# Rows of tokens fetched from DRAM by lists instead of products with one-hot matrices, in the expert loop of a decoder step

## The chip, the cores and the metric

One core of a Trainium2 chip runs the whole kernel. The metric is the device time of one execution in microseconds (us). A core's engines named below are PE (TensorE, the matrix engine), DVE (VectorE), ACT (ScalarE), POOL (GpSimd) and SP (SyncE, which here issues the weights' DMA transfers).

## What is computed

One layer of a hybrid decoder over 288 tokens (256 of a prompt, 32 of samples) of 1024 numbers: a mixer (a convolution and a state-space branch), a layer norm, a mixture of experts and a last layer norm. The change lies in the mixture of experts:

```python
def moe(h, w_r, b_r, w1, b1, w2, b2):
    t = h.reshape(-1, D_MODEL)
    logits = (t @ w_r + b_r).astype(jnp.float32)
    top_val, top_idx = lax.top_k(logits, TOP_K)
    gates = jax.nn.softmax(top_val, axis=-1)
    comb = jnp.einsum('tk,tke->te', gates,
                      jax.nn.one_hot(top_idx, N_EXPERTS, dtype=jnp.float32)).astype(h.dtype)
    out = jnp.zeros_like(t)
    for e in range(N_EXPERTS):
        gu = t @ w1[e] + b1[e]
        g = jnp.minimum(gu[:, :D_FF], SWIGLU_LIMIT)
        up = jnp.clip(gu[:, D_FF:], -SWIGLU_LIMIT, SWIGLU_LIMIT)
        act = g * jax.nn.sigmoid(SWIGLU_ALPHA * g) * (up + 1.0)
        out = out + comb[:, e:e + 1] * (act @ w2[e] + b2[e])
    return out.reshape(shp)
```

All data are float32. An expert's weights are 12 MiB, all experts' 384 MiB. The kernel computes an expert only for the tokens that chose it; 288 tokens with 4 experts each make 1152 pairs of token and expert.

## The kernel before

The first 330 us or so compute the mixer, the norm, `h2` (the tokens' rows after the second modulation, 288 rows of 1024 numbers, in three tiles of 128 partitions) and the router. For each expert the router leaves `posm` (a token's place in the expert's list, or a number that no place has), `comb` (its gate) and `cnt` (how many tokens the expert has).

Then comes the loop over 32 experts `e`, in `moe`. PE, DVE, ACT and POOL run the order in which the code is written. A group `b` is 32 tokens of an expert. The count is loaded into a register of each engine, and nested branches (`rest`) run as many groups as the expert has.

- **Gather** (`onehot`, `gather_mm`, `gather_tr`). DVE compares places with `iota` and makes a one-hot matrix `S` (128 x 3 x 64). PE multiplies `S` by `h2`: six float32 products of 512 columns into PSUM tile `ga`, which the trace shows as 12 records on line L1146. ACT copies `ga` to `gs`, PE transposes it with four products (`gt`, L1157), and ACT copies to `ht0`. This is 64 tokens, so two groups. Groups 2 and 3, and 4 and 5, each have a further gather (`S_1`, `S_2`, into `ht1`) inside the branch.
- **ff1** (`ph1`, L1174 and L1180): groups 1 and up first, inside the branches, then group 0. Tiles `w_0` to `w_7` are the first matrix.
- **Scatter** of the pair of experts before (`sc`, `ss`, L1245 and L1254), only at even `e`.
- **ff2** of groups 1 and up inside the second set of branches (`ph2`, L1209, tiles `w_8` to `w_11`).
- At the expert's end, in this order on PE: gather products of expert `e + 1`, at even `e` the transposes of the gates (`gp`, L1235), transposes `at` of the activations of group 0, transposes `gt` of the gathered rows, ff2 of group 0.
- **Gates** (`gates_a`, `gates_b`): DVE makes a one-hot matrix for a pair of experts in two operations (L1227, L1228), PE transposes it (`gp`) and ACT copies it to `gst`, the left side of the scatter. An expert with three groups or more has such a matrix for its further tokens too (`gp_x`, `gst_x`).

SP issues the weights in the order of use, 1 MiB a transfer, into a ring of 18 buffers (19 later): each transfer waits until PE has done with the tile that lay there (`done`, L1124 for `w_0` to `w_7`, L1126 for the others).

## Time and profile before

| what | before |
|---|---|
| median of 3 runs | 1525.32 us (1520.22 to 1526.88) |
| the profiled execution | 1517.3 us |
| its span, first to last instruction | 1515.2 us |
| PE busy in the span | 1225.3 us (81%) |
| DVE, ACT, POOL busy | 507.8, 336.1, 225.5 us |
| mean granted clock of PE | 0.938 of full speed |
| DMA, mean over the span | 308 GB/s |

The span leaves out what lies before the first and after the last instruction, 2.1 us in the profiled execution. The median of the runs is 8.0 us above the profiled execution. In the trace the expert loop begins at about 326 us with the first gather, its first ff1 product is at 337 us, and its last product is near 1497 us; the rest is the last norm. A row of a timeline gives start, duration, engine, line, operation, output and inputs, sizes, the number of records in it, and in brackets how long the engine sat idle before it and what released it. PEq, DVEq and ACTq are the engines' sequencers: the engine waited at a branch.

### The profile page before, as it was taken

Reading aid. Unit: us, or ns where it says so; the run is one execution under the profiler, and the core shown is the slowest. Engines: PE = TensorE matmul, PEld = TensorE weight load, DVE = VectorE, ACT = ScalarE, POOL = GpSimd, SP = SyncE. Lnnn points to the kernel's source line nnn. Section 1 sums busy time; section 2 is a strip of 40 time slices with the busy share of each in tenths; the row PEclk is TensorE's granted clock in tenths of the full one; section 3 lists DMA queues with packets and bytes.
Section 4 is the critical chain, followed back from the end, with each engine's and each line's share of the span. In section 5 each row is a group of like instructions: output and inputs, shape, how many; then the busy total and the mean of one; then the engine's idle time right before and its main releaser. Section 6 shows DMA issues by size and latency. Waiting matters only on the chain. (4 is left out here: it accounts for less than half of the span.)

```text
span 1515.2 us, 25944 instructions
## 1 busy us (share of the span) xinstructions
PE 1225.3 (81%) x10487; PEld 577.8 (38%) x10487; DVE 507.8 (34%) x910; ACT 336.1 (22%) x703; POOL 225.5 (15%) x181
## 2 busy tenths in 40 slices
PE   4888779967877888879889887788777998788885
PEld 1777668932222233323232332223222242323332
DVE  6799897742202212213122221022211131212233
ACT  3634655421111111111110110111111121111112
POOL 4676955411000000000000000000000000000022
PEclk9999898997999899999999998999989999999998
DMA  9456557468999998886982589998999549985582
GB/s 393 152 223 162 198 181 271 172 229 352 401 412 414 415 415 327 330 337 255 415 335 105 231 341 413 413 416 360 416 412 414 236 186 416 389 358 235 210 321 79
DMA packets 84660, 467.36 MB, mean 308 GB/s; under 512 B 8728, under 2 KB 10096, under 8 KB 45456
## 3 DMA queue, kind: packets, MB, share of 16 engines
q1 hardware_dynamic: 81264, 459.68, 76.4%
q8 instruction: 172, 2.82, 0.7%
q10 hardware_dynamic: 2912, 3.46, 0.7%
q0 software_dynamic: 224, 0.68, 0.3%
q14 instruction: 88, 0.72, 0.1%
HBM read 460.69 MB, written 3.10 MB: 306 GB/s over the span
## 5 line engine op out<-in xcount | busy, mean ns | idle before, releaser
L1382 POOL TENSOR_TENSOR acc.344_2930<-acc.344_2930,w_1.1848_32253 128x1024 f32<-128x1024 f32 x2 | 5.0, 2521 | 1097.1 <-DVEq L1299 1097.1
L1215 ACT COPY ysp.360_2947<-y 32x256 f32<-32x256 f32 x152 | 55.1, 362 | 125.6 <-PE y L1209 112.7
L1174 PE MATMUL gu<-b1h.19_79,sel.17_76 96*32 96x512 bf16 x220 | 22.6, 399 | 70.2 <-PEq L1299 45.2
L1198 ACT COPY at1.355_2942<-at 128x256 f32<-128x256 f32 x32 | 11.9, 372 | 217.4 <-PE at L1196 217.4
L565 DVE SCALAR_TENSOR_TENSOR v.103_626<-cb.73_323,pk.20_88,v.103_626 128x256 f32<-128x256 f32 x60 | 54.6, 911 | 1.5
L1174 PEld LDWEIGHTS <-sel.17_76 96*32 96x32 bf16 x220 | 7.0, 93 | 97.2 <-issue 96.1
L1251 DVE TENSOR_TENSOR acc.344_2930<-acc.344_2930,sc 128x512 f32<-128x512 f32 x60 | 39.8, 684 | 11.9 <-PE sc L1245 11.9
L1251 DVE TENSOR_TENSOR acc.344_2930<-acc.344_2930,sc_x 128x512 f32<-128x512 f32 x28 | 19.3, 688 | 28.1 <-PE sc_x L1245 28.1
L1215 DVE COPY ysp.360_2947<-y 32x256 f32<-32x256 f32 x24 | 10.2, 423 | 40.2 <-ACT ysp.360_2947 L1215 40.2
L1215 DVE COPY ysx.361_2948<-y 32x256 f32<-32x256 f32 x22 | 9.3, 421 | 38.6 <-ACT ysx.361_2948 L1215 38.6
L1158 ACT COPY ht0.358_2945<-gt 128x512 f32<-128x512 f32 x32 | 18.7, 585 | 10.0 <-PE gt L1157 9.9
L1198 ACT COPY at2.356_2943<-at 128x256 f32<-128x256 f32 x14 | 5.2, 372 | 61.9 <-PE at L1196 53.1
L1196 PEld LDWEIGHTS at<-consts.1_57,acts1.349_2936 128*128 128x128 f32 x64 | 6.4, 140 | 27.1 <-issue 27.1
L1196 PE MATMUL at<-consts.1_57,acts0.348_2935 128*128 128x128 f32 x64 | 13.4, 292 | 2.0 <-DVEq L1299 2.0
L1196 PEld LDWEIGHTS at<-consts.1_57,acts0.348_2935 128*128 128x128 f32 x64 | 7.5, 146 | 19.3 <-issue 16.4
L1196 PE MATMUL at<-consts.1_57,acts1.349_2936 128*128 128x128 f32 x64 | 14.0, 301 | 0.0
L1167 DVE TENSOR_SCALAR acts0.348_2935<-gu 128x256 f32<-128x256 f32 x32 | 13.2, 414 | 0.0
L1215 ACT COPY ysx.361_2948<-y 32x256 f32<-32x256 f32 x22 | 8.0, 362 | 22.4 <-PE y L1209 16.9
L1198 ACT COPY at0.354_2941<-at 128x256 f32<-128x256 f32 x32 | 12.3, 383 | 1.5 <-PE at L1196 1.5
L148 ACT COPY yx.131_1005<-y 32x288 f32<-32x288 f32 x10 | 6.9, 688 | 15.7 <-DVE yx.131_1005 L148 10.7
L1245 PE MATMUL sc_x<-ysx.361_2948,gst_x.1801_31355 128*128 128x512 f32 x8 | 6.5, 983 | 4.4 <-PEq L1299 4.4
L1245 PE MATMUL sc_x<-ysx.361_2948,gst_x.1851_32347 128*128 128x512 f32 x8 | 6.7, 1013 | 3.4 <-PEq L1299 3.4
(3185 smaller groups left out, 3004.6 us busy)
## 6 DMA issues: line engine op xcount, KB each, us to landing
wada_0.21_90<-in_w_ada_dram SPq DMA_DIRECT2D x1, 1024.0 KB
wada_1.22_92<-in_w_ada_dram SPq DMA_DIRECT2D x1, 1024.0 KB
wada_2.24_96<-in_w_ada_dram SPq DMA_DIRECT2D x1, 1024.0 KB
wada_3.25_98<-in_w_ada_dram SPq DMA_DIRECT2D x1, 1024.0 KB, 12.7
wada_4.26_100<-in_w_ada_dram SPq DMA_DIRECT2D x1, 1024.0 KB
wada_5.27_102<-in_w_ada_dram SPq DMA_DIRECT2D x1, 1024.0 KB
wada_6.28_104<-in_w_ada_dram SPq DMA_DIRECT2D x1, 1024.0 KB, 19.1
wada_7.29_106<-in_w_ada_dram SPq DMA_DIRECT2D x1, 1024.0 KB
```

What stands on the lines that cost most here:

```text
L148: (e.copy if e is nc.scalar else e.tensor_copy)(out, in_)
L565: V.scalar_tensor_tensor(vt_(j), cb[:, j, k:k + 256], wd[:, k, j:j + 1], vt_(j), op0=ALU.mult, op1=ALU.add)
L1158: nc.scalar.copy(ht, tp)
L1167: nc.vector.tensor_scalar(a, g[:, 256:512], -7.0, 7.0, op0=ALU.max, op1=ALU.min)
L1174: nc.tensor.matmul(o, sel[0:96, e:e + 1].to_broadcast([96, w]), b1v[0:96, :, c, :], start=True, stop=False, tile_position=tp)
L1196: nc.tensor.transpose(tp[:, o:o + P], a[:, h * P:h * P + P], ident)
L1198: nc.scalar.copy(t, tp[:, 256 * m:256 * m + 256])
L1215: (nc.vector.tensor_copy if q % 2 and b else nc.scalar.copy)(ys[r:r + 32, s], y[i, 0:256])
L1245: nc.tensor.matmul(sc, gst[0:W, t * P:t * P + P], ys[0:W, n * 512:n * 512 + 512], start=True, stop=True)
L1251: nc.vector.tensor_tensor(a, a, sc, op=ALU.add)
L1382: nc.gpsimd.tensor_tensor(acc[:, t], acc[:, t], g[:, 0], op=ALU.mult)
```

## The change

The tokens' rows are no longer gathered by products with one-hot matrices. At the end of the mixer `h2` is written to DRAM (`h2d`, three transfers issued by POOL). `lists` makes, with three products of 4 or 2 moving columns and three to five small DVE operations, a table `tab`: for each place its token's number (512, which is out of bounds, where the place is empty) and its gate. `fetch` is one indirect transfer of POOL that reads the rows of `h2d` named by the table, 128 places of 4 KB each; places out of bounds are to be skipped.

A fetch into `gs` serves the first 64 tokens of two experts, an even one and the odd one after it: it is issued at the end of the even expert before, and its rows are transposed (`columns`, 8 products, two copies) at the end of the odd expert before. A fetch into `gsx` serves tokens 64 to 191 of one expert: it is issued for every expert, between `ph1` and `ph2` of the expert before, and `columns_x` transposes 64 of its rows where the further gathers stood. The first pair of experts has no such fetch: it is still gathered by products, now six of 512 columns with a one-hot matrix of 128 places.

The gates' matrix is one DVE compare of `iota` with the table's token numbers, multiplied by the table's gate (`gates`); its transposes and copy are gone. POOL now loads the count and runs all branches too. `gs`, `gsx` and `htx` lie where `h2` lay. The function `more`, for over 192 tokens, is changed as well; no expert has that many here.

```diff
-    def onehot(e, p):
-        s = at_(o_sg if p else o_s, [P, 3, 64], f"S_{e}_{p}")
...
+        s = at_(o_g, [P, 3, P], f"S_{e}_{lo}")
+        if lo is None:
+            o, bc = s.rearrange("p t (n s) -> p t n s", n=2), [P, 3, 2, 64]
+            i, x = iotaj[:, 0:64].unsqueeze(1).unsqueeze(2), posm[:, :, e:e + 2].unsqueeze(3)
...
-    def gather_mm(e, p, s):
...
-    def gather_tr(e, p, gs):
...
+    def lists(e, s, tab, pair):
+
+        nm, n = f"_{e}_{pair}", 4 if pair else 2
+        (tf, ti), ps = tab, pm.tile([P, 512], F32, tag="m", bufs=2, name=f"li_{e}_{pair}")
         for t in range(3):
...
+            nc.tensor.matmul(ps[:, 0:n], s[:, t], cm[:, t].rearrange("p e c -> p (e c)")[:, 2 * e:2 * e + n], start=t == 0, stop=t == 2)
+        nc.vector.tensor_scalar(tf[:, 0:1], ps[:, 1:2], float(NONE), None, op0=ALU.add)
+        nc.vector.tensor_copy(ti, tf[:, 0:1])
+        for i in range(2) if pair else ():
+            nc.vector.tensor_copy(tf[64 * i:64 * i + 64, 1:2], ps[64 * i:64 * i + 64, 2 * i:2 * i + 1])
+        if not pair:
+            nc.vector.tensor_copy(tf[:, 1:2], ps[:, 0:1])
+
+    def fetch(g, tab):
+
+        nc.gpsimd.indirect_dma_start(out=g, out_offset=None, in_=h2d, in_offset=bass.IndirectOffsetOnAxis(ap=tab[1], axis=0),
+                                     bounds_check=287, oob_is_err=False)
+
+    def columns(nm):
+
+        for h in range(2):
+            tp = pm.tile([P, 4, P], F32, tag="m", bufs=2, name=f"gt{nm}_{h}")
+            for i in range(4):
+                nc.tensor.transpose(tp[:, i], gs[:, P * (4 * h + i):P * (4 * h + i) + P], ident)
+            (nc.vector.tensor_copy if h else nc.scalar.copy)(ht[:, 4 * h:4 * h + 4], tp)
+
+    def columns_x(nm, m):
+
+        r = slice(64 * m, 64 * m + 64)
+        tp = pm.tile([P, 8, 64], F32, tag="m", bufs=2, name=f"gt{nm}")
+        for k in range(8):
+            nc.tensor.transpose(tp[:, k], gsx[r, P * k:P * k + P], ident[r, r])
+        nc.scalar.copy(htx[:, :, r], tp)
...
-    def gates_a(o, e, p, n):
...
+    def gates(o, nm, tab):
+
+        g = at_(o, [P, 288], f"gst{nm}")
+        nc.vector.tensor_scalar(g, iotaj[:, 0:288], tab[0][:, 0:1], tab[0][:, 1:2], op0=ALU.is_equal, op1=ALU.mult)
         return g
...
-    def gates_b(o, nm, g, n):
...
             if e % 2 == 0 and e:
-                scatter(f"_{e}", gst, ysp, P)
+                scatter(f"_{e}", gst, ysp)
+            if not last:
+                lists(e + 1, s, tabs[2 + (e + 1) % 2], 0)
+                fetch(gsx, tabs[2 + (e + 1) % 2])
             reg = ph2(e, reg)
-            gates = e == 1 or e and e % 2 == 0
-            if gates:
-                ga = gates_a(o_g, e - e % 2, 0, 2)
             if e:
                 step()
-            if not last:
-                gs = gather_mm(e + 1, 0, s)
-            if gates:
-                gst = gates_b(o_gst, f"_{e}", ga, 2)
+            if e == 1 or e and e % 2 == 0:
+                gst = gates(o_gst, f"_{e}", tabs[j % 2])
+            if e % 2 == 0 and e + 2 < NE:
+                lists(e + 2, onehot(e + 2), tabs[(j + 1) % 2], 1)
+                fetch(gs, tabs[(j + 1) % 2])
...
-            else:
-                gather_tr(e + 1, 0, gs)
+            elif e % 2:
+                columns(f"_{e + 1}")
             ff2(e, 0, ysp, 64 * (e % 2))
```

The first place is the end of an even expert (expert 2) on PE. Here it was, from the last branch to the first product of ff2 of group 0:

```order
L1299 UNCONDITIONAL_BRANCH x3
L1293 TENSOR_LOAD cnt.16_75
L1293 ISA x2
L1289 REGISTER_ALU
L1689 BRANCH_PREFETCH_HINT
L1146 MATMUL ga_0_6000<-h2.13_72,S_0.485_5073 64x512 x6
L1235 MATMUL gp_6009<-consts.1_57,G_0_2.528_5997 128x128 x3
L1196 MATMUL at_6015<-consts.1_57,acts0.348_2935 128x128 x2
L1157 MATMUL gt_0_6019<-consts.1_57,gs_0.529_6007 128x128 x4
L1209 MATMUL y_0_6025<-w_8.469_4683,at0.354_2941 32x256 x8
```

And here it is after the change; `S_None` is the one-hot matrix of the next pair of experts, which DVE makes behind the branch:

```order
L1319 UNCONDITIONAL_BRANCH x3
L1313 TENSOR_LOAD cnt.16_75
L1313 ISA x2
L1309 REGISTER_ALU
L1712 BRANCH_PREFETCH_HINT
L1166 MATMUL li_1_5897<-cm.14_73,S_None.502_5895 128x4 x3
L1230 MATMUL at_5908<-consts.1_57,acts0.349_2945 128x128 x2
L1243 MATMUL y_0_5912<-w_8.456_4631,at0.355_2951 32x256 x8
```

The gather's products, the gates' transposes and the rows' transposes have left this place; a list's three products came, and nothing stands between the transposes `at` and ff2 any more.

The second place is on PE again: the end of an odd expert (expert 1), after the change. Before, it read as expert 2's above without the row of `gp`, with the two rows `tx` of a once-only step ahead.

```order
L1521 MATMUL tx_1_4943<-consts.1_57,xa1.301_2333 128x128 x4
L1230 MATMUL at_4954<-consts.1_57,acts0.349_2945 128x128 x2
L1184 MATMUL gt_0_4958<-consts.1_57,gs0.359_2955 128x128 x4
L1184 MATMUL gt_1_4964<-consts.1_57,gs0.359_2955 128x128 x4
L1243 MATMUL y_0_4970<-w_8.415_3634,at0.355_2951 32x256 x8
```

The transposes of the rows of two experts now stand between `at` and ff2, and wait for the fetch into `gs0`.

The third place is on POOL, between its preparation and the loop's first experts. Before, POOL had nothing from here to the loop's end but two single steps:

```order
L1359 MEMSET acts5.353_2940 128x256
L1299 UNCONDITIONAL_BRANCH x2
L1491 TENSOR_SCALAR xa0.299_2325<-xa0.299_2325,lga.4_63 128x288 x4
L1491 TENSOR_SCALAR xa1.300_2326<-xa1.300_2326,lga.4_63 128x288 x4
L1401 MEMSET ysp.360_2947 64x1024
L1299 UNCONDITIONAL_BRANCH x60
```

After the change, around the end of expert 0:

```order
L1176 DMA gs1.360_2956<-h2d,tab3.366_2962 128x1024
L1319 COMPARE_AND_BRANCH x5
L1319 UNCONDITIONAL_BRANCH x7
L1313 TENSOR_LOAD cnt.16_75
L1176 DMA gs0.359_2955<-h2d,tab1.364_2960 128x1024
L1514 TENSOR_SCALAR xa0.300_2332<-xa0.300_2332,lga.4_63 128x288 x4
```

POOL now has the two fetches and the branches of each half of an expert in its order, so that a fetch stands behind the branches ahead of it.

## Rows read from the trace of the kernel before

**Rows 1.** Stretches: PE, PEld, DVE, ACT, POOL busy, PE clock, DMA share, GB/s.

```profile
337.00:566.00 229.00, 183.00 (x1537) 66.07 (x1537) 41.36 (x93) 33.94 (x82) 5.55 (x9) 0.92 0.98 395
566.00:872.00 306.00, 258.95 (x2440) 97.89 (x2444) 64.94 (x143) 45.90 (x113) 0.00 (x0) 0.95 0.73 292
872.00:1033.00 161.00, 129.14 (x1097) 45.20 (x1089) 27.60 (x61) 22.81 (x56) 0.00 (x0) 0.95 0.98 399
1033.00:1164.00 131.00, 100.70 (x887) 38.11 (x891) 23.96 (x51) 21.24 (x53) 0.00 (x0) 0.92 0.98 398
1164.00:1500.00 336.00, 284.27 (x2610) 105.78 (x2603) 73.55 (x152) 50.60 (x123) 13.69 (x7) 0.95 0.71 283
```

**Rows 2.** Waits of SP's queue, 340 to 1500 us: total, times, longest.

```profile
SPq L1124 <- PE y L1209: 330.2, 76, 34.6
```

**Rows 3.** Line L1124, last ff1 tile of expert 7: issue and landing.

```profile
L1124 SPq DMA_DIRECT2D w_7.714_9607<-in_w_dram x1: 328/328/328, 522.6 to 522.6; - x1
DMA to landing us min/median/max: 19.9/19.9/19.9
```

**Rows 4.** Timeline of PE: first use of that tile, then a further gather.

```profile
544.43 1.04 PE L1180 MATMUL gu<-w_7.714_9607,ht0.358_2945 128*32 128x512 f32 x8
545.41 2.79 PE L1146 MATMUL ga<-h2.13_72,S_1.732_10016 128*64 128x512 f32 x12
```

**Rows 5.** Line L1124, last ff1 tile of expert 19: issue and landing.

```profile
L1124 SPq DMA_DIRECT2D w_7.1302_21409<-in_w_dram x1: 328/328/328, 986.0 to 986.0; - x1
DMA to landing us min/median/max: 20.4/20.4/20.4
```

**Rows 6.** Timeline of PE at 1009 us: first use of that tile.

```profile
1009.14 1.04 PE L1180 MATMUL gu<-w_7.1302_21409,ht0.358_2945 128*32 128x512 f32 x8
```

**Rows 7.** Line L1124, last ff1 tile of expert 24: its issue.

```profile
L1124 SPq DMA_DIRECT2D w_7.1548_26340<-in_w_dram x1: 327/327/327, 1143.8 to 1143.8; - x1
```

**Rows 8.** Timeline of PE at 1169 us: first use of that tile.

```profile
1169.90 1.04 PE L1180 MATMUL gu<-w_7.1548_26340,ht0.358_2945 128*32 128x512 f32 x8
```

**Rows 9.** Stretches two and five, line L1146 alone (12 records a gather).

```profile
566.00:872.00 306.00, 37.41 (x120) 10.25 (x120) 0.95 0.73 292
1164.00:1500.00 336.00, 35.83 (x132) 10.03 (x132) 0.95 0.71 283
```

**Rows 10.** Timeline of PE: transposes of a further gather in expert 29.

```profile
1406.47 0.66 PE L1157 MATMUL gt<-consts.1_57,gs_1.1813_31716 128*128 128x128 f32 x4 [0.73 <-ACT gs_1.1813_31716 L1149]
```

**Rows 11.** One window, 337 to 1500 us, tile gp alone (gates' transposes).

```profile
337.00:1500.00 1163.00, 8.98 (x48) 5.26 (x48) 6.45 (x16) 0.94 0.84 336
```

**Rows 12.** Timeline at the end of expert 20 (even, one group).

```profile
1071.86 2.79 PE L1146 MATMUL ga<-h2.13_72,S_0.1367_22776 128*64 128x512 f32 x12 [1.12 <-PEq L1299]
1071.96 0.56 DVE L1227 TENSOR_TENSOR G_2.1410_23700<-consts.1_57,posm.15_74 128x384 f32<-128x384 f32 x1 [0.73 <-DVEq L1299]
1074.96 0.38 PE L1196 MATMUL at<-consts.1_57,acts0.348_2935 128*128 128x128 f32 x2
1075.51 0.39 ACT L1198 COPY at0.354_2941<-at 128x256 f32<-128x256 f32 x1
1075.96 1.07 PE L1209 MATMUL y<-w_8.1353_22408,at0.354_2941 128*32 128x256 f32 x16
```

**Rows 13.** Timeline at the end of expert 11 (odd, one group).

```profile
730.30 5.39 PE L1146 MATMUL ga<-h2.13_72,S_0.927_13938 128*64 128x512 f32 x12 [4.30 <-issue]
```

**Rows 14.** Timeline of PE at the start of the expert loop.

```profile
326.44 4.49 PE L1146 MATMUL ga<-h2.13_72,S_0.380_2987 128*64 128x512 f32 x12 [3.05 <-DVE S_0.380_2987 L1137]
```

**Rows 15.** Line L1460, Pool's last transfer before the loop: issue and landing.

```profile
L1460 POOL DMA_DIRECT2D b2.346_2932<-in_b_dram x1: 582/582/582, 315.2 to 315.2; - x1
DMA to landing us min/median/max: 6.9/6.9/6.9
```

**Rows 16.** Timeline of PE: last scatter product at expert 6.

```profile
527.08 0.64 PE L1254 MATMUL ss<-ysp.360_2947,gst_4.628_7980 128*32 128x256 f32 x8
```

**Rows 17.** Timeline of PE: transposes at the end of expert 21.

```profile
1101.95 0.66 PE L1157 MATMUL gt<-consts.1_57,gs_0.1460_24686 128*128 128x128 f32 x4 [0.29 <-ACT gs_0.1460_24686 L1149]
```

More of the change, by code (lines that the diff above doesn't have):

```diff
@@ new lines, in more, with part @@
+    def more(e, reg):
+        nm, tab = f"_{e}_m", tabs[4]
+        lists(e, onehot(e, 192), tab, 0)
+        fetch(gsx, tab)
+        def part(m):
+            columns_x(f"{nm}{m}", m)
+            gu = [bank("BC"[i], f"gu{nm}{m}_{i}") for i in range(2)]
+            ff1_mm(e, htx[:, :, 64 * m:64 * m + 64], 64,
+                   [(gu[c // 2][64 * (c % 2):64 * (c % 2) + 64, :].rearrange("p (u n) -> p u n", u=2), (0, 64 * (c % 2))) for c in range(4)])
+            for i in range(2):
+                silu(f"{nm}{m}_{i}", ats[2 + i], gu[i], i)
+            act_tr(f"{nm}{m}", list(zip(ats[2:], ats[:2])))
+            y = bank("B", f"y{nm}{m}")
+            for kt in range(8):
+                c, h = kt // 2, kt % 2
+                for q in range(2):
+                    nc.tensor.matmul(y[64 * q:64 * q + 64, :], ats[c // 2][:, h * P + 64 * (c % 2):h * P + 64 * (c % 2) + 64],
+                                     wt[e][8 + c][:, h, 512 * q:512 * q + 512], start=kt == 0, stop=kt == 7, tile_position=(0, 64 * q))
+            for q in range(2):
+                nc.scalar.copy(ysx[64 * m:64 * m + 64, 512 * q:512 * q + 512], y[64 * q:64 * q + 64, :])
+        part(0)
+        with tc.If(reg > 256):
+            part(1)
+        scatter(nm, gates(o_atx, nm, tab), ysx, e + 1 == NE)
@@ L1320, in f @@
                 with tc.If(reg > 192):
[L1321 removed]
+                    more(e, reg)
         rest(e, reg, "a", f)
@@ L1356, in moe @@
     with tc.manual_schedule(engines={ENG.PE, ENG.DVE, ENG.Activation, ENG.Pool}):
-        gather_tr(0, 0, gather_mm(0, 0, onehot(0, 0)))
-        for t in (acc, accs, ysp[0:64], ysx, *acts[1:]):
+        s = onehot(0)
+        for h in range(2):
+            g = pm.tile([P, 512], F32, tag="m", bufs=2, name=f"ga{h}")
+            for t in range(3):
+                nc.tensor.matmul(g, s[:, t], h2[:, t, 512 * h:512 * h + 512], start=t == 0, stop=t == 2)
+            (nc.vector.tensor_copy if h else nc.scalar.copy)(gs[:, 512 * h:512 * h + 512], g)
+        columns("_0")
+        lists(0, s, tabs[0], 1)
+        lists(0, onehot(0, 64), tabs[2], 0)
+        for t in (gsx, acc, accs, ysp[0:64], ysx, *acts[1:]):
             nc.gpsimd.memset(t, 0.0)
+        fetch(gsx, tabs[2])
         reg = tokens(0)
         for e in range(NE):
-            last = e + 1 == NE
+            last, j = e + 1 == NE, e // 2
             if not last:
-                s = onehot(e + 1, 0)
+                s = onehot(e + 1, 64)
             ph1(e, reg)
```

130 lines of the change are left out of this document (44 added, 86 removed).

## The prediction

> **What bounds the kernel now.** I first read the table of busy time by stretches over the expert loop [rows 1]. Its five stretches are cut where DMA changes: in the first, third and fourth the DMA engines are 98% busy and move 395 to 399 GB/s, in the second and fifth they are at 73% and 71%. PE is busy 956 of the 1163 us from 337 to 1500, about 80% in every stretch, and no other engine comes near it. The waits of SP's queue say who waits for whom where DMA idles: SP waited 330 us in all for PE's ff2 to free a buffer [rows 2]. So in stretches two and five (642 us) the ring is full, PE sets the pace, and a microsecond taken from PE's chain is a microsecond of the total.
>
> In the other three (521 us) the weights come just in time, and I looked at how much PE could move ahead. The last ff1 tile of expert 7 was issued at 522.6 and landed 19.9 us later, at 542.5 [rows 3]; PE first used it at 544.43 [rows 4]: 1.9 us to spare. For expert 19 it is 986.0 + 20.4 = 1006.4 [rows 5] against 1009.14 [rows 6]: 2.7 us. For expert 24 the landing isn't shown; with the same 20.4 us it is 1143.8 + 20.4 = 1164.2 [rows 7] against 1169.90 [rows 8]: 5.7 us. Each of these experts stands at the end of one of the full stretches. Whatever PE saves in such a stretch beyond that slack becomes a wait for weights. This splits the sum in three.
>
> **The change where the ring is full.** The gathers' products were busy 37.41 us in stretch two (10 gathers) and 35.83 us in stretch five (11) [rows 9]. An undisturbed gather took 2.79 us [rows 12], so 21 cost 58.6 us at the full clock. The other 14.6 us are gathers at the half clock, as at the end of expert 11, where the granted clock was at its 1.2 GHz level behind 4.30 us of idle PE and the gather took 5.39 us [rows 13]. I don't count those 14.6: the idle at the branch stays, and the product that comes next takes the slow microseconds over. A further gather also made PE wait 0.73 us for ACT's copy [rows 10]; seven of the nine lie in these stretches: 5.1 us. The gates' transposes are 8.98 us for 16 [rows 11], 0.56 each; 13 of them, further ones included, lie here: 7.3 us. Removed: 58.6 + 5.1 + 7.3 = 71.0 us.
>
> Added there are 19 lists (13 for single experts, 6 for pairs). Three products with a 128-wide load and 2 or 4 columns are not in the trace; the nearest is the gates' three transposes with the same load and 128 columns, 0.56 us. From below nearly nothing, from above 0.56; I take the upper end, 10.6 us. A pair's list stands behind a branch, and its one-hot matrix is made only there: DVE's compare of that size took 0.56 us and started 0.10 us after the gather, which had waited 1.12 us for the branch [rows 12]. With the gates' compare ahead of it, PE waits about 1.1 us, six times: 6.6 us (if the branch delays both alike, as low as 0.5 each). ACT's copy of `at` (0.39 us, with 0.17 between transposes and copy and 0.06 behind it [rows 12]) was hidden by the transposes `gt`; at even experts nothing stands there now, so 0.55 us more, seven times: about 4 us. At odd experts eight transposes cover it, and their total is the same as four at each expert before. A further `columns_x` is eight half-size transposes for four full ones (0.66 us [rows 10]); between nothing and 0.66 more, I take 0.3, so 2 us for seven. For clock lost where less work runs ahead of ff2 I put 4 us (from nothing to the bound of the third rival). Net: 71.0 - 10.6 - 6.6 - 4 - 2 - 4 = **43.8 us gained**.
>
> The Trainium skill would price the rows' transfer lower than I do further down ("DMA: Bandwidth & Descriptors", section "Anatomy of one DMA — SWDGE (gpsimd) path"): 2.0 us plus bytes over 436 GB/s for a transfer that POOL issues, which by an estimate is 3.2 us for 512 KB. By it no fetch is late; by the bound below it, two may be.
>
> **The change where DMA is full.** PE can only move ahead by the slack, 1.9 + 2.7 + 5.7 = 10.3 us. Against it stands the new traffic: 1152 rows of 4 KB, 4.7 MB, at 398 GB/s 11.9 us over the whole loop, of which 521/1163, 5.3 us, falls here. **5 us gained**, between -5 (no use of the slack) and 10.
>
> **The start.** The first gather took 4.49 us [rows 14] with pairs of products side by side in 64 columns each; six full-width ones in sequence are the same columns without that, up to twice as long. Two copies, twice the transposes and two lists follow before the loop begins. I take 5 us lost, from 3 to 8. Writing `h2` to DRAM is POOL's and lies beside this.
>
> **The fetches.** POOL's nearest transfer (128 KB) took 0.6 us to issue and landed in 6.9 us [rows 15]; the far end is a weights' MiB in full DMA, 20.4 us [rows 5]. A pair's fetch is issued about when the gather of an even expert ended, and needed at the transposes of the odd one: between 1074.6 (1071.86 + 2.79) [rows 12] and 1101.95 [rows 17], 27 us, some 24 when the chain is shorter. A further fetch's shortest cover is from the list behind the scatter at 527.7 [rows 16] to 545.41 [rows 4], 17.7 us, and about 15 after the change. With 7 to 12 us from list to landing both hold. At the far end, about 22, the further fetch is 7 us late at experts 7 and 19 and costs up to 14. I take nothing: 0.5 MB at most beside a queue of weights is nearer the small row. POOL's branches come ahead of each fetch; PE met 4.30 us of code loading at one [rows 13], which fits in the cover once, not four times.
>
> **Sum.** 43.8 + 5 - 5 = 43.8 us. Against the profiled execution, 1517.3 us, that is 1473.5; the median of the runs shown is 8.0 higher, so **1481.5 us**.
>
> **Rivals.** (1) *More is gained, because the full stretches aren't a limit.* If weights come earlier once PE frees buffers earlier, the 19 gathers there (53 us at 2.79) and ten gates' transposes (5.6) count too, less 13 lists (7.3), nine waits (10) and eight copies (4.4): 37 in place of 5, so 1450 us. Against it: 98% busy share, 398 GB/s. (2) *Out-of-bounds places are moved too.* 47 fetches of 512 KB are 24.6 MB, 62 us at 398 GB/s, 50 more than counted; 521/1163 of it, 22 us, hits full stretches: 1504 us. The bounds argument speaks against it. (3) *The clock eats the gain.* PE loses dense work right behind the branches where it idles. In [rows 13] the gather itself took the slow stretch; in the new order ff2 of group 0 comes there, 3.6 us at the full clock (four runs like that of `y` [rows 12]), 7.2 at half. If it stays slow at eight more experts of one group in stretches two and five, where it now runs at the full clock, that is 29 us, less the 4 counted: 1506 us. The Trainium skill speaks for this one: "TensorE: Matmul & The Clock Gate", section "HAM oscillation — how this bites in real kernels", says that bursts of products between waits each begin at the slow clock again. The trace agrees for expert 11. (4) *Slower: fetches come late.* Each microsecond by which fetches exceed their cover is paid at 15 pairs and at seven further fetches. With the shortest covers, 15 and 24 us, the gain of 44 is gone at 15 + 44/7, some 21 us from list to landing, more where covers are longer; at 28 us it is 7 x 13 + 15 x 4 = 151 us lost, 107 net: 1632 us. It would take POOL held up by two or three loads of code ahead of each fetch, or a slow building of 128 indirect descriptors; no row shows an indirect transfer.
>
> **How the numbers follow.** Forecast 0.58, (1) 0.12, (2) 0.05, (3) 0.13, (4) 0.12. The forecast's own range is 1466 to 1497: lists at nothing and waits of 0.5 give 14 more, the far end of the fetches and start 17 less. The range reaches to rival 1 on one side and takes in rivals 2 and 3 on the other, leaving out rival 4 and some of rival 1: **1448 to 1510**. A change under 0.5%, 7.6 us, is about what a measurement of this kernel can't tell. Faster by more: the forecast, (1), (2) and most of (3), 0.82; within it 0.06, from (3) and the mild end of (4); slower 0.12.
>
> **What would show it.** Right: SP's waits for PE still long in stretches two and five, DMA at 98% elsewhere with PE waiting for `w_` tiles there, no wait of the transposes `gt` on `gs0` or `gs1`, 4.7 MB in POOL's queue, lists under 0.6 us with about 1.1 us ahead of them at even experts. Wrong: PE waiting for a DMA at `gt` (rival 4), 25 MB in POOL's queue (rival 2), ff2 of group 0 taking 7 us (rival 3), gather time gone in the full stretches without new waits (rival 1).

## The result, and the profile after

The changed kernel takes 1500.96 us in the median of 4 runs (1496.47 to 1506.16), the kernel before 1522.77 us beside it (4 runs, 1517.89 to 1526.88): a ratio of 0.9859, with a 95% interval of 0.9813 to 0.9905. That is 21.8 us faster, where 43.8 were forecast; the forecast of 1481.5 us missed by 19 us, inside its range of 1448 to 1510.

These are lines of the page of the changed kernel: busy time and instructions of PE, the granted clock and DMA's share in 40 slices, POOL's DMA queue (packets, MB, share) and what the page counts at HBM.

```profile
PE 1187.7 (79%) x10262; PEld 600.1 (40%) x10262; DVE 526.1 (35%) x1057; ACT 297.8 (20%) x624; POOL 276.8 (18%) x236
...
PEclk7879889997689889989899997889888998999987
DMA  9455745674799999999694578999999957996682
...
q0 software_dynamic: 7328, 6.55, 1.6%
...
HBM read 485.33 MB, written 4.28 MB: 325 GB/s over the span
```

PE is busy 37.6 us less than before, but the mean granted clock fell from 0.938 to 0.880 in the profiled execution (0.880 to 0.901 in the four runs, against some 0.92 to 0.94 in those of the kernel before). That execution, 1506.16 us, is the slowest of the four, and 6.6 us of it lie ahead of the loop: the first gather begins at 333.04 us instead of 326.44 [rows 14]. The code there hardly changed, and with the same code the gather began at 326.25 us in the trace of the second experiment below, so I don't put this to the change.

The loop is read in the stretches of [rows 1], cut at the same work: the first product of expert 0, the end of ff1 at expert 7, the same product at expert 14, the end of ff1 at expert 19, the start of expert 24, the end. The columns are those of [rows 1].

```profile
355.00:592.00 237.00, 184.60 (x1500) 73.64 (x1492) 46.66 (x129) 26.29 (x66) 16.42 (x20) 0.83 0.96 385
592.00:883.00 291.00, 237.67 (x2379) 97.72 (x2383) 66.13 (x167) 36.60 (x94) 9.89 (x10) 0.92 0.79 313
883.00:1039.00 156.00, 122.62 (x1069) 49.68 (x1061) 31.39 (x87) 17.12 (x44) 7.91 (x8) 0.87 0.97 392
1039.00:1169.00 130.00, 95.72 (x861) 41.74 (x864) 27.93 (x75) 16.62 (x43) 6.92 (x7) 0.86 1.02 412
1169.00:1489.00 320.00, 263.17 (x2529) 102.68 (x2518) 71.72 (x179) 39.98 (x101) 23.01 (x17) 0.94 0.77 309
```

Against 229, 306, 161, 131 and 336 us before, the two stretches with a full ring (second and fifth) gave 15 and 16 us, 31 in all; the third and fourth gave 5 and 1, together 6 of the 8.4 us of slack that the prediction gave them; the first lost 8, and the loop began 11 us later after its first gather. The clock is lower in every one of them, most in those where experts of one group follow each other.

Where the loop begins, ACT's timeline shows one long wait, for a DMA, and PE's shows what that held up:

```profile
340.49 0.58 ACT L1373 COPY gs0.359_2955<-ga 128x512 f32<-128x512 f32 x1 [6.31 <-DMA h2d<-h2.13_72]
...
341.13 4.99 PE L1372 MATMUL ga<-h2.13_72,S_None.388_3004 128*128 128x512 f32 x6 [5.28 <-ACT gs0.359_2955 L1373]
```

`gs0` lies where `h2` lay. The copy of the first gathered half overwrites rows that the transfer into `h2d` is still reading, and waits 6.31 us for it; PE's second half of the gather waits 5.28 us for the copy. The first ff1 product came at 355.20 us, 22.2 us after the gather began; before it was 11.0 (326.44 to 337.45).

The end of expert 20, PE and DVE, answers to [rows 12]:

```profile
1080.14 0.83 PE L1166 MATMUL li<-cm.14_73,S_64.1135_21782 128*128 128x2 f32 x6
...
1082.06 0.43 DVE L1254 TENSOR_SCALAR gst_20.1167_22660<-consts.1_57,tab0.363_2959 128x288 f32<-128x288 f32 x1 [0.63 <-DVEq L1319]
...
1084.52 0.56 DVE L1158 TENSOR_TENSOR S_None.1168_22662<-consts.1_57,posm.15_74 128x384 f32<-128x384 f32 x1 [2.03 <-PEq L1319]
1085.47 1.43 PE L1166 MATMUL li<-cm.14_73,S_None.1168_22662 128*128 128x4 f32 x6 [4.50 <-DVE S_None.1168_22662 L1158]
1086.76 0.67 PE L1230 MATMUL at<-consts.1_57,acts0.349_2945 128*128 128x128 f32 x2
...
1087.89 1.07 PE L1243 MATMUL y<-w_8.1123_21413,at0.355_2951 128*32 128x256 f32 x6 [0.46 <-ACT at0.355_2951 L1232]
1090.12 1.49 PE L1243 MATMUL y<-w_8.1123_21413,at0.355_2951 128*32 128x256 f32 x9 [1.16 <-issue]
```

PE sits idle 4.50 us before the pair's list. DVE's compare, which writes where the list before was read, waited 2.03 us for PE's sequencer to pass the branch, and PE then waits for the compare. (The second experiment shows that at this expert PE would have stood as long without it.) Behind the wait everything is slow: the list takes 1.43 us (the list in the first row took 0.83 at the full clock), `at` 0.67 (0.38 in [rows 12]); the granted clock was 0.50 from 1085.4 to 1091.7 us. At the odd expert 21 the same branch is a wait of 3.81 us without a releaser, and ff2 is slow after it:

```profile
1109.24 0.41 PE L1230 MATMUL at<-consts.1_57,acts0.349_2945 128*128 128x128 f32 x2 [3.81 <-issue]
1109.48 1.35 PE L1184 MATMUL gt<-consts.1_57,gs0.359_2955 128*128 128x128 f32 x8
1110.76 1.94 PE L1243 MATMUL y<-w_8.1159_22334,at0.355_2951 128*32 128x256 f32 x16
1112.47 1.07 PE L1243 MATMUL y<-w_9.1160_22336,at0.355_2951 128*32 128x256 f32 x7
```

A `y` row of 16 records took 1.07 us before [rows 12] and takes 1.94 here. Over the loop the products of ff2 (PE and PEld busy, clock, DMA share, GB/s) are busy 246.12 us against 205.4 before, for the same 3520 records. The rows are the loop now, and the second and the fifth stretch before and now:

```profile
355.00:1489.00 1134.00, 246.12 (x3520) 120.54 (x3520) 0.89 0.87 349
...
566.00:872.00 306.00, 63.89 (x1088) 33.80 (x1088) 0.95 0.73 292
1164.00:1500.00 336.00, 63.63 (x1088) 33.38 (x1088) 0.95 0.71 283
...
592.00:883.00 291.00, 68.75 (x1088) 34.91 (x1088) 0.92 0.79 313
1169.00:1489.00 320.00, 69.06 (x1088) 35.32 (x1088) 0.94 0.77 309
```

Of the 40.7 us more, 10.3 lie in the two stretches with a full ring; the other 30.4 lie where the weights come just in time. From the first to the last product, ff2 of group 0 at the 20 experts of one group took 3.67 us on average before and 5.55 now. The granted clock over it was 1.00 at all 20 before; now it is 0.52 to 0.88 at 17 of them.

The fetches were never late. POOL's 47 indirect transfers, line L1176, took 0.99 us each to issue, and landed:

```profile
DMA to landing us min/median/max: 2.2/8.1/9.2
```

No wait of the transposes `gt` for a transfer appears in PE's waits. Weights do appear there now, as forecast, at expert 7, where 1.9 us of slack stood in [rows 3, 4]; with those at experts 6 and 24 they are 6.0 us in all. At expert 19 there is none. Expert 7:

```profile
569.36 1.07 PE L1214 MATMUL gu<-w_6.616_8739,ht.361_2957 128*32 128x512 f32 x8 [0.40 <-DMA w_6.616_8739<-in_w_dram]
571.88 0.64 PE L1214 MATMUL gu<-w_7.640_9291,ht.361_2957 128*32 128x512 f32 x4 [1.46 <-DMA w_7.640_9291<-in_w_dram]
```

### The profile page after: what moved, and what is told of

It is laid out like the page before. It is cut to its first block, busy times and chain, and to the rows that moved or that the text cites. A ratio compares the mean times of both kernels' runs of the same rounds, so it can differ in the third digit from the quotient of the medians.

```text
span 1504.4 us, 25881 instructions
## 1 busy us (share of the span) xinstructions
PE 1187.7 (79%) x10262; PEld 600.1 (40%) x10262; DVE 526.1 (35%) x1057; ACT 297.8 (20%) x624; POOL 276.8 (18%) x236
## 3 DMA queue, kind: packets, MB, share of 16 engines
q0 software_dynamic: 7328, 6.55, 1.6%
## 5 line engine op out<-in xcount | busy, mean ns | idle before, releaser
L1176 POOL DMA_INDIRECT gs1.360_2956<-h2d,tab3.366_2962 x16 | 15.9, 992 | 567.3 <-DVE tab3.366_2962 L1172 342.7
L1208 PE MATMUL gu<-b1h.19_79,sel.17_76 96*32 96x512 bf16 x220 | 23.9, 423 | 76.9 <-PEq L1319 49.7
L1176 POOL DMA_INDIRECT gs1.360_2956<-h2d,tab2.365_2961 x16 | 16.0, 998 | 344.6 <-DVE tab2.365_2961 L1172 155.0
L1232 ACT COPY at1.356_2952<-at 128x256 f32<-128x256 f32 x32 | 11.9, 372 | 214.1 <-PE at L1230 214.1
L567 DVE SCALAR_TENSOR_TENSOR v.103_627<-cb.73_324,pk.20_89,v.103_627 128x256 f32<-128x256 f32 x60 | 51.7, 861 | 1.5
L1232 ACT COPY at0.355_2951<-at 128x256 f32<-128x256 f32 x32 | 11.9, 372 | 197.4 <-PE at L1230 193.0
L1230 PE MATMUL at<-consts.1_57,acts0.349_2945 128*128 128x128 f32 x64 | 17.8, 372 | 39.3 <-issue 32.0
L1268 DVE TENSOR_TENSOR acc.345_2940<-acc.345_2940,sc 128x512 f32<-128x512 f32 x60 | 39.8, 684 | 11.9 <-PE sc L1262 11.9
L1249 DVE COPY ysp.368_2964<-y 32x256 f32<-32x256 f32 x24 | 10.2, 423 | 52.6 <-ACT ysp.368_2964 L1249 52.6
L1185 DVE COPY ht.361_2957<-gt 128x512 f32<-128x512 f32 x16 | 11.1, 691 | 48.1 <-PE gt L1184 48.1
L1184 PE MATMUL gt<-consts.1_57,gs0.359_2955 128*128 128x128 f32 x128 | 23.7, 344 | 0.3 <-DVE gs0.359_2955 L1373 0.3
L1176 POOL DMA_INDIRECT gs0.359_2955<-h2d,tab1.364_2960 x8 | 7.9, 989 | 73.0 <-DVE tab1.364_2960 L1168 70.3
L1184 PEld LDWEIGHTS gt<-consts.1_57,gs0.359_2955 128*128 128x128 f32 x128 | 20.4, 181 | 1.6 <-issue 0.8
L1176 POOL DMA_INDIRECT gs0.359_2955<-h2d,tab0.363_2959 x7 | 6.9, 989 | 48.1 <-DVE tab0.363_2959 L1168 48.1
```

The lines of the kernel that those rows point to most:

```text
L567: V.scalar_tensor_tensor(vt_(j), cb[:, j, k:k + 256], wd[:, k, j:j + 1], vt_(j), op0=ALU.mult, op1=ALU.add)
L1176: nc.gpsimd.indirect_dma_start(out=g, out_offset=None, in_=h2d, in_offset=bass.IndirectOffsetOnAxis(ap=tab[1], axis=0), bounds_check=287, ...
L1184: nc.tensor.transpose(tp[:, i], gs[:, P * (4 * h + i):P * (4 * h + i) + P], ident)
L1185: (nc.vector.tensor_copy if h else nc.scalar.copy)(ht[:, 4 * h:4 * h + 4], tp)
L1208: nc.tensor.matmul(o, sel[0:96, e:e + 1].to_broadcast([96, w]), b1v[0:96, :, c, :], start=True, stop=False, tile_position=tp)
L1230: nc.tensor.transpose(tp[:, o:o + P], a[:, h * P:h * P + P], ident)
```

## The experiments

The theory after this reading: half of the forecast gain is lost in two places, the start (the copy that waits for the transfer out of `h2`) and the clock (ff2 takes over the slow microseconds that the gathers had, and more of them); the even experts' wait is a loss that was forecast. The rivals: the gain is held by DMA or eaten by extra traffic (HBM counts 24.6 MB more), or PE's own branches end last whatever stands there. How far the theory held is said behind the experiments.

| kernel | median us | ratio to before (95%) |
|---|---|---|
| changed | 1500.96 | 0.9859 (0.9813 to 0.9905) |
| 1 first rows elsewhere | 1490.74 | 0.9787 (0.9755 to 0.9820) |
| 2 pair's list behind ff2 | 1486.25 | 0.9771 (0.9735 to 0.9806) |
| 3 ten products before the branch | 1571.02 | 1.0319 (1.0271 to 1.0367) |
| 4 all places in bounds | 1520.49 | 0.9993 (0.9969 to 1.0016) |
| 5 both edits, 1 and 2 | 1479.58 | 0.9731 (0.9695 to 0.9767) |
| 6 three products before the branch | 1480.16 | 0.9730 (0.9705 to 0.9755) |
| 7 gather's work put back | 1533.15 | 1.0076 (1.0047 to 1.0104) |
| 8 edits 1, 2 and 6 | 1460.91 | 0.9587 (0.9553 to 0.9621) |
| 9 a second filler | 1511.15 | 0.9931 (0.9908 to 0.9955) |
| 10 the kernel before with the filler of 6 | 1557.44 | 1.0222 (1.0186 to 1.0258) |
| 11 fetch just before its use | 1558.27 | 1.0222 (1.0183 to 1.0261) |

The medians of the kernel before lay between 1518.92 and 1524.09 us in these sets.

**1. The first pair's rows are copied elsewhere.**

```diff
-            (nc.vector.tensor_copy if h else nc.scalar.copy)(gs[:, 512 * h:512 * h + 512], g)
-        columns("_0")
+            (nc.vector.tensor_copy if h else nc.scalar.copy)(ysx[:, 512 * h:512 * h + 512], g)
+        columns("_0", ysx)
```

> The changed kernel, with one edit: the rows of the first pair of experts, gathered by products, are copied into the buffer of the further groups' results instead of into gs0, which lies over h2. Theory (the start costs more than forecast because ACT's copy into gs0 must wait until the transfer that writes h2 to DRAM has read that place): the copy no longer waits, the second gather's products follow the first at once, and the loop begins 5 to 7 us earlier; 1494 to 1496 us against 1501. Rival (the branch's code load and the half clock set the start anyway): at most 2 us, 1499 to 1501.

It took 1490.74 us, 10 less, where the theory had 5 to 7. PE's timeline at the start:

```profile
327.37 6.89 PE L1372 MATMUL ga<-h2.13_72,S_None.388_3004 128*128 128x512 f32 x12 [1.47 <-DVE sm.343_2926 L1093]
334.10 0.60 PE L1184 MATMUL gt<-consts.1_57,ysx.369_2965 128*128 128x128 f32 x4
...
343.14 1.93 PE L1214 MATMUL gu<-w_0.370_2966,ht.361_2957 128*32 128x512 f32 x8
```

The two halves of the gather now run as one, and from the gather to the first ff1 product it is 15.8 us instead of 22.2: 6.4 us, the copy's wait. The median shows a little more; medians of the same kernel before differ by 5 us between sets, so the rest can't be told from that. The remaining 4.8 us over the 11.0 of before are what the forecast had put at 5.

**2. The pair's list moves behind ff2.**

```diff
             if e % 2 == 0 and e + 2 < NE:
-                lists(e + 2, onehot(e + 2), tabs[(j + 1) % 2], 1)
-                fetch(gs, tabs[(j + 1) % 2])
+                s = onehot(e + 2)
...
             ff2(e, 0, ysp, 64 * (e % 2))
+            if e % 2 == 0 and e + 2 < NE:
+                lists(e + 2, s, tabs[(j + 1) % 2], 1)
+                fetch(gs, tabs[(j + 1) % 2])
```

> The changed kernel, with the products of a pair's list (and the fetch behind them) moved behind ff2 of group 0; its one-hot matrix is still made behind the branch, so that PE does not wait for it. Theory (PE's wait at the end of even experts is the branch and then DVE's compare, about 1.05 us more than before at each of 15 experts): 15 x 1 us less idle, and the full gain only where the ring is full, so 6 to 15 us less, about 1491 us. Rival (PE's own branch ends last there, the compare lies beside it): the idle moves to the transposes of the activations, 0 to 3 us less, 1498 to 1501.

1486.25 us, 14.7 less: the theory's upper end. PE's waits for `S_None`, 47.2 us in all in the changed kernel, are 3.7, while those of `at` at the branch rose from 36.9 to 62.2: 18 us less idle. Only half of this is what the theory meant. Expert by expert, nine of the 15 pairs' waits (1.7 to 3.6 us each) are shorter by 1.1 us on average: there DVE's compare ended last. At the other six (3.6 to 5.9 us each, 26.6 in all) nothing came back; they are 27.5 us without the list. Expert 20, shown above, is one of them:

```profile
1058.57 0.66 PE L1230 MATMUL at<-consts.1_57,acts0.349_2945 128*128 128x128 f32 x2 [4.45 <-issue]
```

There the rival holds: PE's own branch ends last. The other 8 us less idle lie at odd experts, where the edit takes nothing away. Why isn't shown; that code is fetched at other moments, as in the next experiment, is a possible cause.

**3. and 6. Filler in the wait at the branch.** In both, products whose result nobody reads stand in front of PE's branch between the halves of an expert. First ten bf16 products:

```diff
+        f = pm.tile([P, 512], F32, tag="m", bufs=2, name=f"fi{nm}")
+        for i in range(n):
+            nc.tensor.matmul(f, sel[0:96, 0:1].to_broadcast([96, P]), b1v[0:96, :, i % 4, :], start=True, stop=True)
...
                 fetch(gsx, tabs[2 + (e + 1) % 2])
+            filler(f"_{e}", 10)
             reg = ph2(e, reg)
```

> The changed kernel, with ten bf16 products of 512 columns, whose result nobody reads, in front of PE's branch between the two halves of each of the 32 experts: 2.1 us of work at the full clock, 4.3 at half. Theory (the gain is eaten by the half clock that follows the idle at this branch, where the gather's products stood before): the products run while the branch loads its code, the granted clock rises from 0.88 to over 0.91, ff2 of group 0 falls from about 5.0 to about 3.8 us where one group is all, and the time falls by 10 to 25 us, to 1476 to 1491. Rival (the clock costs little, work counts): 32 x 1.0 to 2.1 us more, 1530 to 1565.

1571.02 us, 70 more, against the theory, and more than its rival allowed. Yet ff2 of group 0 was back at 3.95 us. The waits of PE tell where the time went (total, times, longest):

```profile
PE gu L1208 <- PEq L1325: 67.5, 24, 4.6
PE gu L1214 <- issue: 40.8, 21, 3.8
...
PE at L1230 <- issue: 12.9, 11, 1.2
```

In the changed kernel these were 49.7 (24 times), 7.2 (3 times) and 32.6 (10 times). The wait at the branch between the halves (`at`) did shrink; but 18 new waits of up to 3.8 us came in the middle of ff1, at no branch. What PE waits for there can be read from the DMA packets. PE's code comes in packets of 16 KB on a queue of its own. In the page of the changed kernel, packets, MB and share of that queue are:

```profile
q8 instruction: 167, 2.74, 0.7%
```

All 21 waits of ff1 without a releaser end 1.2 to 1.6 us after such a packet has come in. In the changed kernel it is so too: the eight long waits of `at` without a releaser (3.7 to 4.2 us) end 2.5 to 2.7 us after one, and the 14 waits over 1 us for the sequencer at ff1's branch (L1319) 1.8 to 2.0. The 12 waits of the same products for ACT's copies, for comparison, end anywhere from 2.2 to 12.1 us after one. So these waits are for code, and twenty more instructions an expert (a load and a product each) moved some of them into ff1. The same was then tried with three float32 products. In the trace they are six loads and six products, so twelve instructions by the same count, not the six that the expectation names:

```diff
+        for i in range(n):
+            nc.tensor.matmul(f[:, 0:320], ident, iotaj[:, 0:320], start=True, stop=True)
...
+            filler(f"_{e}", 3)
```

> The changed kernel with filler again in front of the branch between the halves of an expert, now three float32 products of 320 columns, some 1.6 us of work in six instructions instead of twenty; nobody reads the result. With ten products ff2 of group 0 was back at 4.0 us from 5.6, yet the time rose by 70 us, and waits of PE without a releaser and at branches rose by some 50 us in the trace. Theory (the loss came from the number of instructions: more code, more loads that PE waits for): those waits stay near the changed kernel's, ff2 of group 0 stays near 4 us, the filler lies in the wait at the branch, and the time is 1475 to 1500 us. Rival (the filler itself is paid in full): 1530 or more.

1480.16 us: 20.8 us faster than the changed kernel by doing 60 us of useless work (32 x 1.86 us). Expert 21 again, PE's timeline, to be held against the rows of the changed kernel above:

```profile
1079.95 0.83 PE L1166 MATMUL li<-cm.14_73,S_64.1173_22808 128*128 128x2 f32 x6
1080.64 1.86 PE L1284 MATMUL fi<-consts.1_57 128*128 128x320 f32 x6
1083.81 0.41 PE L1230 MATMUL at<-consts.1_57,acts0.349_2945 128*128 128x128 f32 x2 [1.31 <-issue]
1084.06 1.04 PE L1184 MATMUL gt<-consts.1_57,gs0.359_2955 128*128 128x128 f32 x8
1085.03 1.07 PE L1243 MATMUL y<-w_8.1159_22414,at0.355_2951 128*32 128x256 f32 x16
```

From the filler's start to `at` it is 3.2 us with 1.86 of filler in it; without filler it was a wait of 3.81. Behind the 1.31 us of idle that is left, ff2 runs at 1.07 us a row. Over the loop ff2's products are busy 223.10 us instead of 246.12:

```profile
349.00:1466.00 1117.00, 223.10 (x3520) 113.84 (x3520) 0.93 0.88 354
```

The rival falls, since the filler is not paid in full, but it isn't free: PE's idle time fell by 40.7 us for 59.6 of filler, so some 19 us were paid, and PE's other products, which are busy 42 us less, met that twice over. The 20.8 us are what is left of both (23 in the profiled executions). The waits for code elsewhere stayed as they were (at the next expert's branch 52.6 us for 49.7, in ff1 4.9 for 7.2), so code that happened to lie better is not what gave them.

**4. All places in bounds.**

```diff
-        nc.vector.tensor_scalar(tf[:, 0:1], ps[:, 1:2], float(NONE), None, op0=ALU.add)
+        nc.vector.tensor_scalar(tf[:, 0:1], ps[:, 1:2], float(NONE), 287.0, op0=ALU.add, op1=ALU.min)
```

> The changed kernel, with empty places of a list naming row 287 instead of 512, which is out of bounds (their gate is 0, so the result is the same): every fetch moves 128 rows, 24.6 MB in all instead of 4.7 MB. Theory (places out of bounds cost next to nothing now): 19.9 MB more at 398 GB/s are 50 us of transfer, of which the three full stretches' share, 15 to 23 us, is paid: 1516 to 1524 us, and POOL's queue moves 26 MB instead of 6.6. Rival (the chip reads the rows out of bounds anyway, as the page's HBM figure, 24.6 MB above that of before, may suggest): no change, 1499 to 1503 us.

1520.49 us, 19.5 more, in the middle of the theory's 15 to 23; PE's waits for weights grew from 6.0 to 17.3 us in the trace. POOL's queue:

```profile
q0 software_dynamic: 7328, 26.51, 4.7%
...
HBM read 485.33 MB, written 4.28 MB: 323 GB/s over the span
```

It moved 26.51 MB in as many packets as the changed kernel's 6.55. So places out of bounds cost a packet but no row, and rival 2 of the prediction falls, with its price (22 us) about right. The page's HBM line is the same in both kernels, 24.6 MB above that of before, as if each of the 47 fetches moved 128 rows: it doesn't see that rows were skipped.

**5. Both edits together.** The diffs of 1 and 2.

> The changed kernel with both edits: the first pair's rows copied elsewhere than over h2, and the pairs' lists made behind ff2. Theory (two separate losses, of the start and of the even experts' ends): the gains of the two alone, 10 and 15 us, add up: 1474 to 1480 us; PE's waits for weight tiles at experts 7, 19 and 24 grow by some us, since the full stretches have no slack left. Rival (one loss, or DMA holds all that is gained ahead of experts 7, 19 and 24): 1484 to 1490.

1479.58 us: 21.4 less than the changed kernel, where the two alone gave 24.9. They add up within what the medians can tell. PE's waits for weights grew from 6.0 to 10.4 us in the trace.

**7. The gather's work is put back behind the branch.**

```diff
+        for t in range(3):
+            for c in range(2):
+                nc.tensor.matmul(f[64 * c:64 * c + 64, :], ident[:, 0:64], wt[e][8 + t][:, 0, 512 * c:512 * c + 512],
+                                 start=t == 0, stop=t == 2, tile_position=(0, 64 * c))
...
+            if not last:
+                as_before(e)
```

> The changed kernel with the gather's work put back where it stood, at each expert's end but the last: six float32 products of 512 columns in pairs of 64, on an ff2 tile and with an unread result. The lists, fetches and transposes stay as changed. By the sum of the prediction the 31 products in place of the gathers cost 2.79 us each where the ring is full (14 of them there, 39 us) and the slack of some 10 us elsewhere: about 49 us, 1550. By the clock theory they take over the slow microseconds that ff2 has now (about 1.8 us at each of 20 experts of one group), and lie beside DVE's compare at even experts: 49 less 25 to 35, 1515 to 1525 us, with ff2 of group 0 at 3.7 to 4.

1533.15 us, 32.2 more: between the two, 8 us above the clock theory's range and 17 below the plain sum. Two rows, of the put-back products alone and of ff2's alone, over the loop:

```profile
350.00:1512.00 1162.00, 114.60 (x372) 32.68 (x372) 0.92 0.85 341
...
350.00:1512.00 1162.00, 203.94 (x3520) 108.12 (x3520) 0.92 0.85 341
```

114.6 us of work cost 32. In the profiled executions, whose spans differ by 27 us, PE's other products are busy 64 us less, 42 of it in ff2 (246.12 to 203.94), and PE is idle 24 us less. ff2 of group 0 is back at 3.67 us at the 20 experts of one group, as it was before the change. This is the change's own main term measured backwards: 31 gathers weren't worth their busy time.

**8. Edits 1, 2 and the filler of 6 together.**

> The changed kernel with the first rows copied elsewhere, the pairs' lists behind ff2, and the filler of three float32 products (unread) in front of the branch between the halves of an expert. Theory (three separate losses: start, even experts' ends, clock): 1480 of the first two alone, less most of the 21 us that the filler gave alone, 1460 to 1468 us; the weights of experts 7, 19 and 24 take some of it, with PE's waits for tiles above 15 us. Rival (the filler had only filled the wait for the pairs' compare, which is gone here): 1476 to 1484.

1460.91 us, within the theory's 1460 to 1468: 40 us less than the changed kernel, 61 less than before, ratio 0.9587. The three losses are separate, and the rival falls. PE's waits for weights are 11.9 us (5.4 at expert 7, 6.5 at expert 24), not above 15 as expected. This is the fastest of these kernels.

**9. A second filler, behind ff2.**

```diff
             done(e, range(8, 12))
+            if not last:
+                filler(f"_{e}_e", 3)
```

> As the kernel with both edits and one filler, and a second filler of three such products behind ff2 of group 0, ahead of the next expert's first branch, where PE waits 2 to 5 us too and then begins ff1 at half clock. Theory (the same mechanism at the other branch): ff1 of group 0 alone falls from about 9 towards 7.6 us, 0.5 to 1 us at each of 31 experts, of which the ring lets half count: 8 to 15 us less than with one filler, 1448 to 1458. Rival (that branch's wait begins only after PE has finished, or ACT's copies end last there): the filler is paid, 0 to 25 us more, 1464 to 1490.

1511.15 us, 50 more than with one, and more than the rival allowed. The wait at the next expert's branch did shrink, from 66.7 us in 24 waits to 35.8 in 25, the second of these rows:

```profile
PE at L1230 <- issue: 46.1, 20, 5.0
PE gu L1208 <- PEq L1325: 35.8, 25, 3.5
...
PE gu L1214 <- issue: 13.5, 6, 3.9
PE y L1243 <- issue: 12.2, 11, 2.1
```

but those of `at` rose from 20.9 to 46.1 us and new ones came within ff1 and ff2. For 58 us of filler PE's idle time fell by only 10. The theory fails at this place. The waits that end right behind a packet of code, read as above, were 75 us with one filler at these four places, 62.5 of them at the next expert's branch; with two they are 89: 27.6 at that branch, 35.6 at `at`, 13.5 in ff1 and 12.2 in ff2. So the waits for code moved to other places. That they follow from where the instructions come to lie is the likely reason; no run tries that by itself.

**10. The kernel before with the filler of 6.**

> The kernel before, with the same filler of three products in front of its branch between the halves of an expert. Theory (before, the gather took the slow microseconds: 135 us busy for 40 gathers of 2.79, 23 us too many): the gathers run at the full clock, up to 23 us less, of which what lies where the ring is full counts, 10 to 18 us: 1502 to 1513 us against 1519 to 1524. Rival (the gather warms the clock by itself, at no loss that counts): 0 to 20 us more.

1557.44 us, 35 more than before, where the rival had allowed 20. 60.2 us of filler took the 40 gathers of the loop only from 135.1 to 129.3 us, and the waits of `ga` at the branch from 64 us (30 times) to 53 (32 times): 60 - 6 - 11 = 43 us left to pay, about what was measured. In the changed kernel there was more to fill, 84 us at `at` and the pairs' lists together, and ff2 behind it to gain; here ff2 was at the full clock already. That the length of the wait decides is a reading that fits both kernels, and no run shows it by itself: before, 13 of the waits were over 3 us too. Some of them fell to 1.2 us behind the filler (experts 9, 17 and 21), while others rose from some 1.3 to 3 or 4 (experts 1 and 5).

**11. The fetch just before its use.**

```diff
                 lists(e + 2, onehot(e + 2), tabs[(j + 1) % 2], 1)
+            if e % 2 and not last:
                 fetch(gs, tabs[(j + 1) % 2])
```

> The changed kernel, with a pair's fetch issued at the end of the odd expert, right ahead of the transposes that need it, instead of one expert earlier; the list is made where it was. Theory (the transfers are hidden only by their cover, rival 4 of the prediction): landing took 8.1 us in the middle and 9.2 at most behind an issue of 1 us; some 3 us of it lie beside PE's wait at the branch, so 5 to 8 us of idle PE ahead of the transposes at each of 15 pairs, 75 to 120 us: 1576 to 1621. Rival (full stretches have PE wait anyway, or a short fetch lands within the branch's wait): 1500 to 1540.

1558.27 us, 57 more, less than the theory's 75 but far above its rival. PE's waits:

```profile
PE gt L1184 <- DMA gs0.359_2955<-h2d,tab1.364_2960: 50.7, 6, 10.5
PE gt L1184 <- DMA gs0.359_2955<-h2d,tab0.363_2959: 46.6, 5, 12.1
```

97 us of idle at 11 of 15 pairs; at the other four PE's waits name no transfer. The time rose by less, since PE's idle time rose by 67 us in all: the waits for code at the next expert's branch fell from 49.7 to 33.8 us, and those for weights, 6.0 us, are gone. One expert of cover is what hides the fetch, and rival 4 of the prediction had its mechanism right and only its lateness wrong.

## Why the prediction was right in part

The range held, in part because it was wide enough for rival 3 (1506 us). The forecast's own range of 1466 to 1497, which its terms make 1467 to 1498, missed. By stretches of the two profiled executions the forecast is 26 us short (22 by the medians): 31 us in place of 43.8 where the ring is full, 2 lost in place of 5 gained where DMA is full, and 11.2 lost in place of 5 at the start.

**What bounds the loop** was right. The stretches with a full ring gave the gain, and SP still waits there for PE's ff2 (118 and 88 us). The third and fourth gave 6 us together, within their slack; at expert 7 PE now waits for `w_6` and `w_7`. Rival 1 (1450 us) falls with that.

**Where the ring is full,** the first step that failed is the term of the lists. 19 lists were put at 0.56 us "from above", 10.6 us in all. They took 17.5:

```profile
592.00:883.00 291.00, 9.00 (x57) 8.15 (x57) 0.92 0.79 313
1169.00:1489.00 320.00, 8.52 (x60) 7.67 (x60) 0.94 0.77 309
```

A list took 0.83 us at the full clock and up to 1.44 at half. The bound from the gates' three transposes was no bound: those make three records ([rows 11]: 48 for 16), a list's three products make six, each with a load, and with 2 columns a record still took 0.25 us behind a load of 0.19. The 6.9 us between are as much as PE's busy time misses there: it fell by 42.4 us, where the forecast's terms make 49.3.

The second is the wait. PE's idle time there rose by 11.4 us (47.0 to 53.3 and 51.7 to 56.8 by [rows 1] and the rows above), where the sum has 5.5: 6.6 at even experts and 4 for the copy of `at`, less the 5.1 of the further gathers. About 1.1 us a pair for DVE's compare is what experiment 2 gave back at nine of 15 experts; at the other six PE now waits longest, for its own code (26.6 us, against 13.2 before), and the forecast had counted on this idle time to stay. The copy of `at` was right, though its three times add up to 0.62 us and not 0.55: PE waited 0.44 us for it, 16 times.

**The clock** had its mechanism right and, where the ring is full, about its size. The forecast kept the gathers' 14.6 slow us as lost ("the product that comes next takes the slow microseconds over") and put 4 us more. ff2 takes 10.3 us more there, as shown above, ff1 takes 8.9 and `at` 1.5: 20.7 for the 18.6 of the sum. Before, a gather stood between the branch and ff2, and ff2 ran at the full clock. Now only short products do (lists, `at` or `gt`), and ff2 runs at the 1.2 GHz level for much of its length. That is the mechanism of rival 3, which I had at 0.13, but not its price: it had 29 us of ff2 in these two stretches. Experiment 6 shows that the slow clock can be bought off, 20.8 us over the loop with some 19 us of filler paid; it doesn't show that the sum was wrong by as much.

The rule that spoke for it, of the Trainium skill ("TensorE: Matmul & The Clock Gate", section "HAM oscillation — how this bites in real kernels"), that products between waits begin slow each time, agrees with the trace: a `y` row takes 1.94 us behind 3.81 us of idle at expert 21 and 1.07 behind 1.31 us of idle in experiment 6.

**Where DMA is full,** the step that failed is "PE can only move ahead by the slack": PE also fell behind. The first stretch lost 8 us, 6.7 of them between the first ff1 products of experts 0 and 1 (355.2 to 399.5, against 337.4 to 375.0). There ff2 took 8.8 us (3.7 before), and the first of the single steps behind it 6.28 instead of 4.46. The weights' DMA stood still there from 391 to 398 us (2 GB/s), so PE set the pace, and the time was not made up.

**The start** was mis-sized: 5 us forecast, 11.2 measured (22.2 against 11.0 from the gather to the first ff1 product), because "Writing `h2` to DRAM is POOL's and lies beside this" was wrong. The transfer reads what the next copy overwrites, and experiment 1 gave the 6.4 us back.

**The fetches** were right: 8.1 us to landing in the middle, 9.2 at most, no wait, and 4.7 MB of rows (6.55 MB in POOL's queue, less the 0.68 of before and the 1.18 of `h2`). The Trainium skill's fit ("DMA: Bandwidth & Descriptors", section "Anatomy of one DMA — SWDGE (gpsimd) path") gives, as an estimate, 3.2 us for a full fetch; these, most of them with few rows in bounds, took 8.1, so here the measurement decides and the row of [rows 15], 6.9 us, was the better guide. Rival 2 is refuted by experiment 4.

What stays open: this account is read from one execution of each kernel, and no run prices the lists, the waits for code or the first stretch by itself. Of these misses only the start was taken away alone, by experiment 1.

## What to carry to other kernels

Work that is removed behind a stall of the matrix engine has a second price: it was also what brought the clock back, and the products that follow now pay for that. Look at what will stand right behind the idle, and try a few wide products with an unread result inside it. Here this gained at one place of one kernel and lost at two others, so measure it each time, and see in the trace whether waits for code have moved. A bound on a small operation has to come from one with as many records. When a buffer is laid over one that a transfer still reads, the transfer is on the path, whoever issues it.

## What was not expected of the hardware

- PE waits for its code, and more instructions moved these waits to places without a branch: ten filler products an expert turned 3 waits within ff1 (7.2 us) into 21 (40.8 us), each ending 1.2 to 1.6 us behind a 16 KB packet of code, and a second filler of three products added 50 us in all.
- An indirect transfer of 128 places issued in 0.99 us of POOL and landed in 2.2 to 9.2 us beside a full weights' queue; places out of bounds made packets but moved no row (6.55 against 26.51 MB in the same 7328 packets), while the page's HBM figure counted them.
- Useless work made the kernel faster: 60 us of it, 41 of them in PE's idle time, took 20.8 us off.
